# Modulation sums: 32x32 turns on VectorE and stacked identities in place of TensorE transposes, gates through DRAM, small rows on GpSimd's queue

## The chip, the cores and the metric

One core of one Trainium2 chip runs the kernel. The time is the device time of one execution in microseconds (us), median of the runs; the profile is of one further execution. Engines: PE is TensorE, PEld its weight loads, DVE is VectorE, ACT is ScalarE, POOL is GpSimd, SP is SyncE, which here only issues transfers (DMAs).

## The reference

Two blocks on a sequence of 256 rows of 1024 columns, fp32. The first is a gated mixer (a short convolution and a forgetting attention) with a feed-forward part. The second has two layers (block-wise attention, then differential attention, each with a feed-forward part), and every layer is modulated by a vector c:

```
c_act = silu(c)                                  # 1 x 1024
for i in range(2):
    mod = c_act @ ada_w[i] + ada_b[i]            # 1024 x 6144 weights
    sh_a, sc_a, g_a, sh_f, sc_f, g_f = split(mod, 6)
    h = rms_norm(x, norm_g[i, 0]) * (1 + sc_a) + sh_a
    x = x + g_a * rms_norm(attention(h), norm_g[i, 1])
    h = rms_norm(x, norm_g[i, 2]) * (1 + sc_f) + sh_f
    x = x + g_f * rms_norm(swiglu(h), norm_g[i, 3])
```

So there are 12 modulation vectors of 1024 numbers: four shifts and four scales, wanted with one channel per partition, and four gates, wanted as a row of 1024 that is the same on all 128 partitions.

## The kernel before, in words

The kernel works on two halves of 128 rows. Weights stream through three buffers (`raws`) on SP's queue; ScalarE rounds each 128x512 piece to fp32r (`hi`), VectorE subtracts it from the original (`lo`), and TensorE makes three products per piece (`triple`, or `turned_product` in the feed-forward parts, where the weights are the stationary side). Sixteen slots hold converted pieces. The order of the work is written by a planner (`Order`): it keeps a simulated time, runs tasks that yield until a due time, and pins the instructions of each engine, and of each DMA queue, in the order in which it emits them. All matmuls and transposes are emitted by `Order.mm` (L145) and `Order.tr` (L151), all other engines' work by `Lane` (L89), all DMAs by `Order.dma` (L137).

The modulation runs beside all this (`ada`, L656): its weights come through two buffers of their own (`araws`), and VectorE accumulates weight times `c_act` into a 128x512 tile `asum`, two instructions for each of 96 pieces. After eight of them a half vector (512 columns) is summed up except over the partitions, and `ada_finish` (L623) does that. For a shift or a scale, PE transposes the four 128x128 blocks, and VectorE reduces the bank along its free axis into `fm`; for a scale a second instruction adds one and multiplies the norm gain. For a gate, the tile is split into hi and lo, which takes one of the sixteen slots, two products with a matrix of ones sum it over the partitions and spread it to all of them, and VectorE multiplies it into `gated[..].tile`, into which `load_gain` (L607) has loaded the norm gain, broadcast to all partitions. That happens twice for each vector (`cc` 0 and 1). `chain` (L552) is the consumer: it waits for the marks in `ada_done`, and its first product reads the gate's tile. There are two such gain tiles.

At the start (L479 to L500) SP loads the first half of x, the first weight tile in four pieces, the second half of x, then in `later` seven small sets of rows (c, the convolution's weights, five norm gains; 4 to 6 KB each), then the next weight tiles. The first gain rows (`first_rows`) come on ScalarE's queue. PE turns the rows to columns later (`turn_rows`). A row tile of these is one of the four `ep` tiles, which the attention heads use too. An unused tile (`PAD_END`) keeps the addresses behind it where they are.

Of the kernel before, what the change touches and what calls it, by code (L numbers as in the profile page):

```python
# [12 lines left out]
F32 = mybir.dt.float32  # L13
F32R = mybir.dt.float32r
AF = mybir.ActivationFunctionType
OP = mybir.AluOpType
AX = mybir.AxisListType
# [3 lines left out]
P = 128  # L21
D = 1024
# [11 lines left out]
STOCK = 9  # L34
ADA_START, ADA_EARLY, ADA_LATE = 30.0, 5.5, 8.0
HEADS_1, HEADS_2 = 9.0, 2.0
PAD_END = 104
FIRST_DMA, SLOW_BYTES = 1.9, 2.2e6
RATE, SLOW_RATE = 360e3, 270e3
WARM = 6  # L40
# [178 lines left out]
def block_kernel(ctx: ExitStack, tc: tile.TileContext, a: dict, onehot: bass.AP, out: bass.AP):  # L219
    nc = tc.nc  # L220
    o = Order(tc)
    A, V, G = o.A, o.V, o.G
# [4 lines left out]
    dram = ctx.enter_context(tc.tile_pool(name="dram", bufs=1, space=DRAM))  # L227

    def ring(pool, name, n, shape, dtype=F32):
        return Ring([pool.tile(shape, dtype, name=f"{name}{i}") for i in range(n)])  # L230

    def small(name, shape, dtype=F32):
        return cst.tile(shape, dtype, name=name)

    banks = ring(psum, "bank", 8, [P, 512])
    raws = ring(cst, "raw", 3, [P, 2048])
    araws = ring(cst, "araw", 2, [P, 1024])
    slots = Ring([(small(f"hi{i}", [P, 512], F32R), small(f"lo{i}", [P, 512], F32R)) for i in range(16)])
    st = ring(cst, "st", 4, [P, 528])
    ch = ring(cst, "ch", 3, [P, 512])  # L240
    ep = ring(cst, "ep", 4, [P, 384])
    gains = ring(cst, "gain", 2, [P, D])
    asum = ring(cst, "asum", 2, [P, 512])
# [119 lines left out]
    def split(hi, lo, src, after=0.0):  # L363
        t = A.activation(hi, src, AF.Copy, after=after)
        return V.tensor_sub(lo, src, hi.bitcast(F32), after=t)
# [76 lines left out]
    vec = {}  # L442

    def rows(*wanted, lane=None):
        n = sum(k for _, _, k in wanted)
        got, e, r = small(f"cols{n}", [P, n]), o.hold(ep), 0
        t = e[:n, :P]
        for name, ap, k in wanted:
            arrival = o.dma(t[r:r + k, :], ap, lane)
            vec[name] = got[:, r:r + k]  # L450
            r += k
        return got, e, arrival

    def turn_rows(got, e, arrival, mark):
        yield arrival
        n = got.shape[1]
        t = e[:n, :P]
        tp = yield from o.get(banks)
        r = o.tr(tp[:, :n], t, ident[:n, :n])
        ep.give(e, r)  # L460
        yield r
        mark.t = V.tensor_copy(got, tp[:, :n])
        banks.give(tp, mark.t)

    def load_x(h):
        for n in range(2):
            c = slice(n * 512, (n + 1) * 512)
            x_in[h][n].t = o.dma(x[h][:, c], xin[h][:, c])
# [3 lines left out]
    def stay_warm():  # L472

        b = banks.take()
        for _ in range(WARM):
# [5 lines left out]
    first_rows = rows(("mix_pre", a["norm_mix_pre"].rearrange("l (k p) -> (l k) p", p=P), 8), lane=A)  # L481
    issue_raw()
    load_x(1)
    later = rows(("c", a["c_2"].rearrange("l (k p) -> (l k) p", p=P), 8),
                 ("conv", a["conv_w"].rearrange("l t (k p) -> (l t k) p", p=P), 12),
                 ("ffn_pre", a["norm_ffn_pre"].rearrange("l (k p) -> (l k) p", p=P), 8),
                 *((("g", l, i), a["norm_g_2"][l, i].rearrange("(k p) -> k p", p=P), 8) for l in range(2) for i in (0, 2)))
    ident = small("ident", [P, P])
    make_identity(nc, ident)
    tri = small("tri", [P, P])  # L490
    nc.vector.memset(tri, 1.0)
    ones_r = small("ones_r", [P, P], F32R)
# [2 lines left out]
    nc.gpsimd.affine_select(tri, tri, pattern=[[1, P]], compare_op=OP.is_ge, fill=0.0, base=0, channel_multiplier=-1)  # L495
    mhalf = small("mhalf", [P, 1])
    nc.vector.memset(mhalf, -0.5)
    pre_mark = Mark()
    o.fill = fill
    o.now = START  # L500
# [106 lines left out]
    def load_gain(src, gain):  # L607
        gain.tile = yield from o.get(gains)
        gain.load.t = o.dma(gain.tile, src.to_broadcast([P, D]))


    fm = [small(f"fm{l}", [P, 4, 8]) for l in range(2)]
# [3 lines left out]
    ada_done = {one: [Mark(), Mark()] for one in ada_order}  # L616
    gated = {one: Gain() for one in ada_order if one[1][0] == "g"}
# [2 lines left out]
    c_mark = Mark()  # L620
    c_act = small("c_act", [P, 8])

    def ada_finish(l, what, cc, sums, r):  # L623
        yield r
        c = slice(cc * 512, (cc + 1) * 512)
        if what[0] == "g":
            yield from o.until(gated[l, what].load)
            pair = yield from o.get(slots)
            hv, lv = pair
            r = split(hv, lv, sums)  # L630
            asum.give(sums, r)
            yield r
            tp = yield from o.get(banks)
            o.mm(tp, ones_r, hv, True, False)
            r = o.mm(tp, ones_r, lv, False, True)
            slots.give(pair, r)
            yield r
            dst = gated[l, what].tile[:, c]
            r = V.tensor_mul(dst, dst, tp)
        else:  # L640
            tp = yield from o.get(banks)
            for j in range(4):
                r = o.tr(tp[:, j * P:(j + 1) * P], sums[:, j * P:(j + 1) * P], ident)
            asum.give(sums, r)
            yield r
            i = {"sh_a": 0, "sc_a": 1, "sh_f": 2, "sc_f": 3}[what]
            dst = fm[l][:, i, cc * 4:cc * 4 + 4]
            r = V.reduce_sum(dst, tp.rearrange("p (k c) -> p k c", c=P), axis=AX.X)
            if what[1] == "c":
                yield r  # L650
                g = vec["g", l, 0 if what == "sc_a" else 2][:, cc * 4:cc * 4 + 4]
                r = V.scalar_tensor_tensor(dst, dst, 1.0, g, op0=OP.add, op1=OP.mult)
        banks.give(tp, r)
        ada_done[l, what][cc].t = r

    def ada():  # L656
        yield from o.until(c_mark)
        pieces = [(l, what, cc, k0) for l, what in ada_order for cc in range(2) for k0 in range(0, 8, 2)]
        loaded, t0 = [], o.now
        for i in range(len(pieces) + 1):  # L660
            if i < len(pieces):
                l, what, cc, k0 = pieces[i]
                c0 = parts_of.index(what) * D + cc * 512
                if k0 == 0:
                    if what[0] == "g" and cc == 0:
                        o.spawn(load_gain(a["norm_g_2"][l, 1 if what == "g_a" else 3].unsqueeze(0), gated[l, what]))
                    sums = yield from o.get(asum)
                    r = G.memset(sums, 0.0)
                    yield r
                    ba = o.dma(sums[0:1, :], a["ada_b_2"][l:l + 1, c0:c0 + 512])  # L670
                t = yield from o.get(araws)
                arrival = o.dma(t.rearrange("p (k c) -> p k c", c=512),
                                a["ada_w_2"][l].rearrange("(k p) c -> p k c", p=P)[:, k0:k0 + 2, c0:c0 + 512])
                loaded.append((l, what, cc, k0, t, max(arrival, ba), sums))
            if i:
                l, what, cc, k0, t, arrival, s = loaded.pop(0)
                yield max(arrival, t0 + i * ADA_EARLY)
                while (o.urgent or V.free > o.now + SLACK or
                       pos["lo"] - pos["first"] < STOCK and o.now < t0 + i * ADA_LATE):
                    yield o.now + 0.2  # L680
                for k in range(2):
                    r = V.scalar_tensor_tensor(s, t[:, k * 512:(k + 1) * 512], c_act[:, k0 + k:k0 + k + 1], s,
                                               op0=OP.mult, op1=OP.add)
                    yield r - 0.3
                araws.give(t, r)
                if k0 == 6:
                    o.spawn(ada_finish(l, what, cc, s, r), r)


    def scope(**kinds):  # L690

        stack, got = ExitStack(), {}
        for name, (n, shape, dtype) in kinds.items():
            got[name] = ring(stack.enter_context(tc.tile_pool(name=name, bufs=1, reuse_waits="tile")), name, n, shape, dtype)
        return stack, got
# [77 lines left out]
        yield from rstd(rs0[h], parts)  # L773
        rs_mark[h].t = V.tensor_scalar(rsq[h], rs0[h], 0.125, None, op0=OP.mult)

    o.spawn(turn_rows(*first_rows, pre_mark))
    for h in range(2):
        o.spawn(turn_x(h))

# [5 lines left out]

    small("pad_end", [P, PAD_END])
    phase, sc = scope(qp=(4, [P, 4, 256], F32), gp=(8, [P, 512], F32),
# [203 lines left out]
    for k0 in (0, 4):  # L991
        for h in range(2):
            t = product(b0[h], hT, h, range(k0, k0 + 4), us_0[k0:k0 + 4], hm, k0 == 0, k0 == 4)
# [5 lines left out]
    group(take(2), 260, keep_gb, None)  # L999
    o.spawn(gates_of_c())  # L1000
    o.spawn(ada(), ADA_START)
    group(take(2), 512, keep_gc, None)
    group(take(2), 512, make_z, None)
# [30 lines left out]
    for n in range(2):  # L1034
        us = take(1)
        o.wait(ya_mark)
        for h in range(2):
            ps = o.hold(banks)
            t = product(ps, yaT, h, range(4), us)
# [22 lines left out]
    for h in range(2):  # L1062
        for n in range(2):
            ps = o.hold(banks)
            t = product(ps, ybT, h, range(4), ub[n])
# [366 lines left out]
```

## Time and profile before

| what | value |
|---|---|
| median of 3 runs (lowest to highest) | 979.92 us (978.97 to 983.75) |
| the profiled execution's own time, its span | 979.98 us, 978.3 us |
| PE, PEld, DVE, ACT, POOL busy | 968.3, 808.5, 771.0, 619.5, 34.8 us |
| mean granted TensorE clock | 0.999 |
| bytes moved by DMA | 227.23 MB, 232 GB/s |

A busy share is an average over stages. Matmuls are pipelined, so the durations of neighbours overlap; what one costs is seen in the distance between starts. An x2 behind a row says that two equal instructions were merged into it. A name such as `bank<-hTb,hi` is the tile written and the tiles read.

### The profile page before, as it was taken

The numbers are of one execution on the slowest core, as the hardware profiler recorded it, in microseconds if no ns is written. First come the engines' busy times: TensorE is split into PE (matmuls) and PEld (weight loads), VectorE is DVE, ScalarE is ACT, GpSimd is POOL, SyncE is SP. The second block draws the span as 40 slices with busy tenths as digits, with TensorE's granted clock in tenths as the row PEclk, the third lists the DMA queues.
The fourth block names the chain that finished last, engine by engine and source line by source line (L and its number), as shares of the span: only waits on it lengthen the run. The fifth ranks groups of instructions, "written<-read, shape, count | busy, mean of one in ns | idle before, by whom it ended". The sixth has DMA issues, their size and how long they took to land.

```text
span 978.3 us, 14495 instructions
## 1 busy us (share of the span) xinstructions
PE 968.3 (99%) x4986; PEld 808.5 (83%) x4986; DVE 771.0 (79%) x1582; ACT 619.5 (63%) x1390; POOL 34.8 (4%) x65
## 2 busy tenths in 40 slices
PE   9999999999999999999999999999999999999997
PEld 6888778888888888888878888888887888888886
DVE  6789789889999977886899989957686787565642
ACT  6756676775555647776775555547788796564631
POOL 1000000000000001000000000001000100000000
PEclk9999999999999999999999999999999999999999
DMA  7977787679988985866769998954442567646501
GB/s 248 343 240 262 260 280 249 217 232 321 350 289 283 300 269 198 278 214 185 246 217 331 307 327 280 315 202 165 171 161 86 185 203 256 217 158 214 166 23 44
DMA packets 143637, 227.23 MB, mean 232 GB/s; under 512 B 6087, under 2 KB 79028, under 8 KB 143564
## 3 DMA queue, kind: packets, MB, share of 16 engines
q1 hardware_dynamic: 143548, 226.30, 69.3%
q8 instruction: 39, 0.64, 0.3%
q14 instruction: 34, 0.28, 0.1%
q10 hardware_dynamic: 16, 0.00, 0.0%
HBM read 225.22 MB, written 2.63 MB: 233 GB/s over the span
## 4 chain that ended last, share of the span: by engine, by line
PE 89%; DMA 4%; DVE 2%; issue 2%; ACT 1%; SPq 0%; POOL 0%; DVEq 0%; POOLq 0%; ACTq 0%
PE bank L145 85%; PE bank L151 4%; DMA raw<-in_w_gate_up_dram 1%; DMA araw<-in_ada_w_dram 1%; DMA raw<-in_w_down_dram 1%; DVE asum L89 1%; ACT hi L89 1%; DMA x<-in_x_dram 1%; DVE lo L89 1%; SPq L137 0%; DVE st L89 0%; DMA raw<-in_w_in_dram 0%; DVE wp L89 0%; DVE x L89 0%; ACT junk L89 0%
## 5 line engine op out<-in xcount | busy, mean ns | idle before, releaser
L89 DVE TENSOR_TENSOR lo<-raw,hi 128x512 fp32r<-128x512 f32 (+1 forms) x494 | 320.8, 677 | 28.6 <-ACT hi L89 24.5
L89 ACT ACTIVATE hi<-raw 128x512 fp32r<-128x512 f32 (+1 forms) x494 | 289.6, 619 | 49.1 <-PE bank L145 20.5
L145 PE MATMUL bank<-hi,hTb 128*128 128x512 f32 (+1 forms) x840 | 265.6, 389 | 0.5 <-ACT hTb L89 0.5
L145 PE MATMUL bank<-hTb,hi 128*128 128x512 f32 x640 | 203.8, 397 | 0.1
L145 PEld LDWEIGHTS bank<-hi,hTb 128*128 128x128 f32 x840 | 153.9, 188 | 30.7 <-issue 1.5
L145 PE MATMUL bank<-lo,hTb 128*128 128x512 f32 (+1 forms) x420 | 163.2, 389 | 0.0
L145 PE MATMUL bank<-hi,pair 128*128 128x512 f32 x496 | 162.5, 392 | 0.0
L89 DVE SCALAR_TENSOR_TENSOR asum<-araw,c_act,asum 128x512 f32<-128x512 f32 x192 | 143.1, 746 | 2.3 <-DMA araw<-in_ada_w_dram 2.1
L145 PEld LDWEIGHTS bank<-hTb,lo 128*128 128x128 f32 x640 | 119.9, 188 | 27.8 <-issue 0.3
L145 PE MATMUL bank<-hTb,lo 128*128 128x256 f32 x640 | 127.2, 280 | 0.0
L145 PEld LDWEIGHTS bank<-hi,pair 128*128 128x128 f32 x496 | 92.7, 188 | 18.6 <-issue 0.2
L89 ACT ACTIVATE wp<-raw 128x512 fp32r<-128x512 f32 x150 | 90.0, 626 | 24.8 <-PE bank L145 16.6
L89 ACT ACTIVATE st<-bank 128x256 f32<-128x256 f32 (+1 forms) x104 | 36.3, 397 | 106.1 <-PE bank L145 105.6
L145 PEld LDWEIGHTS bank<-hTb,hi 128*128 128x128 f32 x640 | 99.8, 189 | 3.2 <-issue 1.0
L89 DVE TENSOR_TENSOR wp<-raw,wp 128x512 fp32r<-128x512 f32 x150 | 98.8, 685 | 3.8 <-ACT wp L89 3.8
L145 PE MATMUL bank<-hTb,wp 128*128 128x512 f32 (+1 forms) x512 | 97.8, 337 | 0.0
L145 PE MATMUL bank<-lo,pair 128*128 128x512 f32 x248 | 97.3, 392 | 0.0
L145 PEld LDWEIGHTS bank<-hTb,wp 128*128 128x128 f32 x512 | 81.5, 188 | 11.5
L145 PEld LDWEIGHTS bank<-lo,hTb 128*128 128x128 f32 x420 | 79.0, 188 | 14.3 <-issue 0.5
L145 PE MATMUL bank<-wp,pair 128*128 128x512 f32 x336 | 84.5, 391 | 0.0
L89 DVE TENSOR_TENSOR st<-st,bank 128x256 f32<-128x256 f32 x96 | 39.8, 416 | 42.5 <-ACT st L89 42.4
L145 PEld LDWEIGHTS bank<-wp,pair 128*128 128x128 f32 x336 | 61.9, 188 | 12.1
(133 smaller groups left out, 868.9 us busy)
## 6 DMA issues: line engine op xcount, KB each, us to landing
araw<-in_ada_w_dram SPq DMA_DIRECT2D x96, 512.0 KB
raw<-in_ffn_w_in_dram SPq DMA_DIRECT2D x88, 512.0 KB
raw<-in_w_gate_up_dram SPq DMA_DIRECT2D x44, 512.0 KB
raw<-in_ffn_w_out_dram SPq DMA_DIRECT2D x22, 1024.0 KB
raw<-in_w_in_dram SPq DMA_DIRECT2D x16, 1024.0 KB
raw<-in_moba_w_qkv_dram SPq DMA_DIRECT2D x12, 1024.0 KB
raw<-in_diff_w_qkv_dram SPq DMA_DIRECT2D x12, 1024.0 KB
raw<-in_w_down_dram SPq DMA_DIRECT2D x11, 1024.0 KB
```

The source lines that it names most:

```text
L89: self.order.pin(self, fn(out, *args, **kw))
L145: self.pin(self.pe, self.nc.tensor.matmul(out, lhsT, rhs, start=start, stop=stop, skip_group_check=shared))
L151: self.pin(self.pe, self.nc.tensor.transpose(out, src, ident))
```

## The change

`ada_finish` now collects both halves of a vector. VectorE turns every 32x32 block of the 128x512 sum in place of its block (`transpose` into a tile of the ring `st`) and reduces the 32 columns of every block: that leaves 16 columns per half, and in a tile `fold` of 32 columns the sums over each quarter of 32 partitions. When both halves are there, four small products sum the quarters. For a shift or a scale the stationary side is `stacked` (four identities of 32x32 above one another, built at the start by four copies) and the moving side eight columns of `fold`; the result has the channels on the partitions. For a gate, the sides are exchanged, the result is eight rows of 128. These are multiplied by the norm gain's eight rows (loaded into an `ep` tile), written to a DRAM tile `gate_d`, and read back, broadcast to all partitions, into the gain tile. `load_gain` is not called for gates any more, and for the gates no slot and no ones are used. There is one `fold` tile, so one vector is in it at a time.

The seven small loads of `later` go to GpSimd's queue and stand behind the making of the identity and the masks; `turn_rows` of the first gain rows is due at once and no longer at the planner's arrival of the load. `PAD_END` goes from 104 to 40 for the 64 columns of `stacked` and `fold`.

```diff
-PAD_END = 104
+PAD_END = 40
...
-    later = rows(("c", a["c_2"].rearrange("l (k p) -> (l k) p", p=P), 8),
...
     ident = small("ident", [P, P])
     make_identity(nc, ident)
+    stacked = small("stacked", [P, 32])
+    for q in range(4):
+        nc.vector.tensor_copy(stacked[q * 32:(q + 1) * 32], ident[q * 32:(q + 1) * 32, q * 32:(q + 1) * 32])
...
     nc.vector.memset(mhalf, -0.5)
+    later = rows(("c", a["c_2"].rearrange("l (k p) -> (l k) p", p=P), 8),
+                 ("conv", a["conv_w"].rearrange("l t (k p) -> (l t k) p", p=P), 12),
+                 ("ffn_pre", a["norm_ffn_pre"].rearrange("l (k p) -> (l k) p", p=P), 8),
+                 *((("g", l, i), a["norm_g_2"][l, i].rearrange("(k p) -> k p", p=P), 8) for l in range(2) for i in (0, 2)),
+                 lane=G)
...
+    folded = Ring([(small(f"fold{i}", [P, 32]), Mark(), Mark()) for i in range(1)])
+    fold_of = {}
+    gate_d = dram.tile([4, D], F32, name="gate_d")
+
     def ada_finish(l, what, cc, sums, r):
         yield r
-        c = slice(cc * 512, (cc + 1) * 512)
+        if not cc:
+            fold_of[l, what] = yield from o.get(folded)
+            for m in fold_of[l, what][1:]:
+                m.t = None
+        while (l, what) not in fold_of:
+            yield o.now + 0.1
+        one = fold_of[l, what]
+        z = yield from o.get(st)
+        r = V.transpose(z[:, :512], sums)
+        asum.give(sums, r)
+        yield r
+        r = V.reduce_sum(one[0][:, cc * 16:(cc + 1) * 16], z[:, :512].rearrange("p (b j) -> p b j", j=32), axis=AX.X)
+        st.give(z, r)
+        one[1 + cc].t = r
+        if not cc:
+            return
+        yield from o.until(*one[1:])
+        by_q = one[0].rearrange("p (k q) -> p q k", q=4)
         if what[0] == "g":
-            yield from o.until(gated[l, what].load)
-            pair = yield from o.get(slots)
-            hv, lv = pair
-            r = split(hv, lv, sums)
...
-            o.mm(tp, ones_r, hv, True, False)
-            r = o.mm(tp, ones_r, lv, False, True)
...
-            r = V.tensor_mul(dst, dst, tp)
+            e = yield from o.get(ep)
+            row = e[:8, :P]
+            yield o.dma(row, a["norm_g_2"][l, 1 if what == "g_a" else 3].rearrange("(k p) -> k p", p=P)) + 1.0
+        tp = yield from o.get(banks)
+        for q in range(4):
+            c = slice(q * 32, (q + 1) * 32)
+            if what[0] == "g":
+                r = o.mm(tp[:8, c], by_q[:, q], stacked, True, True)
+            else:
+                r = o.mm(tp[c, :8], stacked, by_q[:, q], True, True)
+        folded.give(one, r)
+        yield r
+        if what[0] == "g":
+            i = (0 if what == "g_a" else 1) + 2 * l
+            r = V.tensor_mul(row, tp[:8, :P], row)
+            banks.give(tp, r)
+            yield r + 3.0
+            r = o.dma(gate_d[i:i + 1].rearrange("o (k p) -> (o k) p", p=P), row)
+            ep.give(e, r)
+            yield r + 6.0
+            gain = gated[l, what]
+            gain.tile = yield from o.get(gains)
+            r = o.dma(gain.tile, gate_d[i:i + 1].to_broadcast([P, D]))
         else:
-            tp = yield from o.get(banks)
-            for j in range(4):
-                r = o.tr(tp[:, j * P:(j + 1) * P], sums[:, j * P:(j + 1) * P], ident)
...
             if what[1] == "c":
+                r = V.scalar_tensor_tensor(fm[l][:, i], tp[:, :8], 1.0, vec["g", l, 0 if what == "sc_a" else 2],
+                                           op0=OP.add, op1=OP.mult)
+            else:
+                r = V.tensor_copy(fm[l][:, i], tp[:, :8])
+            banks.give(tp, r)
+        for m in ada_done[l, what]:
+            m.t = r
...
-                    if what[0] == "g" and cc == 0:
-                        o.spawn(load_gain(a["norm_g_2"][l, 1 if what == "g_a" else 3].unsqueeze(0), gated[l, what]))
...
-    o.spawn(turn_rows(*first_rows, pre_mark))
+    o.spawn(turn_rows(*first_rows[:2], o.now, pre_mark))
```

## Rows read from the trace of the kernel before

**Rows 1.** Page, part 1: busy us (share of the span) xinstructions.
```profile
PE 968.3 (99%) x4986; PEld 808.5 (83%) x4986; DVE 771.0 (79%) x1582; ACT 619.5 (63%) x1390; POOL 34.8 (4%) x65
```

**Rows 2.** Page, part 4: the chain that ended last, by engine.
```profile
PE 89%; DMA 4%; DVE 2%; issue 2%; ACT 1%; SPq 0%; POOL 0%; DVEq 0%; POOLq 0%; ACTq 0%
```

**Rows 3.** Waits of PE: waited for, us in total, times, longest.
```profile
PE bank L476 <- DVE junk L470: 1.3, 1, 1.3
PE bank L151 <- DVE st L89: 0.6, 1, 0.6
```

**Rows 4.** Timeline of PE: start, us, engine line op out<-in shapes.
```profile
325.97 0.60 PE L151 MATMUL bank<-ident,asum 128*128 128x128 f32 x4
...
327.11 0.63 PE L145 MATMUL bank<-hTb,hi 128*128 128x512 f32 x2
...
327.80 0.63 PE L145 MATMUL bank<-hTb,hi 128*128 128x512 f32 x2
```

**Rows 5.** Timeline of PE around a gate's products with ones.
```profile
593.43 0.62 PE L145 MATMUL bank<-hTb,hi 128*128 128x512 f32 x2
...
594.60 0.63 PE L145 MATMUL bank<-hTb,wp 128*128 128x512 f32 x2
```

**Rows 6.** Groups by line and form: busy us, mean ns, idle before.
```profile
L151 PE MATMUL bank<-ident,asum 128*128 128x128 f32 x64 | 9.6, 273 | 0.6 <-DVE st L89 0.6
L145 PE MATMUL bank<-hi,ones_r 128*128 128x512 f32 x8 | 3.2, 395 | 0.0
L89 DVE TENSOR_REDUCE fm<-bank 128x4 f32<-128x512 f32 x16 | 11.0, 688 | 3.1 <-PE bank L151 2.9
L89 DVE TENSOR_TENSOR lo<-asum,hi 128x512 fp32r<-128x512 f32 x8 | 5.5, 691 | 5.1 <-ACT hi L89 4.8 <-PE bank L145 0.4
L89 DVE TENSOR_TENSOR gain<-gain,bank 128x512 f32<-128x512 f32 x8 | 5.5, 682 | 1.2 <-PE bank L145 1.2
```

**Rows 7.** Timeline of PE, fp32 products with 8 moving columns.
```profile
38.88 0.28 PE L145 MATMUL bank<-logf,ones_r 128*128 128x8 f32 x2
39.02 0.37 PE L145 MATMUL bank<-logf,tri 128*128 128x8 f32 x2
39.25 0.48 PE L145 MATMUL bank<-hi,hTb 128*128 128x512 f32 x1
```

**Rows 8.** Timeline of PE, fp32 products with 128 moving columns.
```profile
760.60 1.05 PE L145 MATMUL bank<-gp,ptp 128*128 128x128 f32 x8
761.41 0.48 PE L145 MATMUL bank<-hi,hTb 128*128 128x512 f32 x1
```

**Rows 9.** Windows: stretch, us, busy us of PE, PEld, DVE, ACT, POOL; clock, DMA.
```profile
200.00:350.00 150.00, 149.66 (x791) 127.62 (x789) 138.21 (x254) 86.24 (x184) 3.69 (x7) 1.00 0.89 300
500.00:650.00 150.00, 149.91 (x790) 127.81 (x789) 139.14 (x253) 87.12 (x184) 3.16 (x6) 1.00 0.88 298
```

**Rows 10.** Timeline of DVE: a gate's last product, its first reader.
```profile
608.64 0.68 DVE L89 TENSOR_TENSOR gain<-gain,bank 128x512 f32<-128x512 f32 x1
...
774.43 0.68 DVE L89 TENSOR_TENSOR ch<-bank,gain 128x512 f32<-128x512 f32 x1
```

**Rows 11.** Timeline of SP's queue at the start.
```profile
5.48 0.27 SPq L137 DMA_DIRECT2D ep<-in_norm_ffn_pre_dram  x1
6.84 2.26 SPq L137 DMA_DIRECT2D ep<-in_norm_g_dram  x4
9.46 2.81 SPq L137 DMA_DIRECT2D raw<-in_w_in_dram  x6
```

**Rows 12.** Timeline of the start; in brackets idle before, and what ended it.
```profile
5.22 0.17 DVE L89 COPY cols<-bank 128x8 f32<-128x8 f32 x1 [3.76 <-PE bank L151]
...
12.26 0.63 ACT L89 ACTIVATE hi<-raw 128x512 fp32r<-128x512 f32 x1 [0.73 <-DMA raw<-in_w_in_dram]
...
13.86 0.50 PE L145 MATMUL bank<-hi,hTb 128*128 128x512 f32 x1 [0.54 <-ACT hTb L89]
```

**Rows 13.** Timeline of POOL at the start.
```profile
14.10 0.66 POOL L89 TENSOR_TENSOR rs<-tiny,mhalf 128x1 f32<-128x1 f32 x1 [10.47 <-DVE tiny L89]
```

More of the change, by code (lines that the diff above doesn't have):

```diff
@@ L483, in block_kernel @@
     load_x(1)
-    later = rows(("c", a["c_2"].rearrange("l (k p) -> (l k) p", p=P), 8),
-                 ("conv", a["conv_w"].rearrange("l t (k p) -> (l t k) p", p=P), 12),
-                 ("ffn_pre", a["norm_ffn_pre"].rearrange("l (k p) -> (l k) p", p=P), 8),
-                 *((("g", l, i), a["norm_g_2"][l, i].rearrange("(k p) -> k p", p=P), 8) for l in range(2) for i in (0, 2)))
     ident = small("ident", [P, P])
     make_identity(nc, ident)
+    stacked = small("stacked", [P, 32])
+    for q in range(4):
+        nc.vector.tensor_copy(stacked[q * 32:(q + 1) * 32], ident[q * 32:(q + 1) * 32, q * 32:(q + 1) * 32])
     tri = small("tri", [P, P])
@@ L621, in block_kernel @@
     c_act = small("c_act", [P, 8])
+    folded = Ring([(small(f"fold{i}", [P, 32]), Mark(), Mark()) for i in range(1)])
+    fold_of = {}
+    gate_d = dram.tile([4, D], F32, name="gate_d")
     def ada_finish(l, what, cc, sums, r):
         yield r
-        c = slice(cc * 512, (cc + 1) * 512)
-        if what[0] == "g":
-            yield from o.until(gated[l, what].load)
-            pair = yield from o.get(slots)
-            hv, lv = pair
-            r = split(hv, lv, sums)
-            asum.give(sums, r)
-            yield r
-            tp = yield from o.get(banks)
-            o.mm(tp, ones_r, hv, True, False)
-            r = o.mm(tp, ones_r, lv, False, True)
-            slots.give(pair, r)
-            yield r
-            dst = gated[l, what].tile[:, c]
-            r = V.tensor_mul(dst, dst, tp)
-        else:
-            tp = yield from o.get(banks)
-            for j in range(4):
-                r = o.tr(tp[:, j * P:(j + 1) * P], sums[:, j * P:(j + 1) * P], ident)
-            asum.give(sums, r)
-            yield r
+        if not cc:
[16 more added lines that the diff above has]
+        by_q = one[0].rearrange("p (k q) -> p q k", q=4)
+        if what[0] == "g":
+            e = yield from o.get(ep)
[21 more added lines that the diff above has]
+            r = o.dma(gain.tile, gate_d[i:i + 1].to_broadcast([P, D]))
+        else:
@@ L646, in ada_finish @@
             i = {"sh_a": 0, "sc_a": 1, "sh_f": 2, "sc_f": 3}[what]
-            dst = fm[l][:, i, cc * 4:cc * 4 + 4]
-            r = V.reduce_sum(dst, tp.rearrange("p (k c) -> p k c", c=P), axis=AX.X)
             if what[1] == "c":
[L650 to L654, printed above, removed]
+                r = V.scalar_tensor_tensor(fm[l][:, i], tp[:, :8], 1.0, vec["g", l, 0 if what == "sc_a" else 2],
+                                           op0=OP.add, op1=OP.mult)
+            else:
+                r = V.tensor_copy(fm[l][:, i], tp[:, :8])
```

## The prediction

> **What bounds the kernel now.** I read four views in this order. The page's first part: TensorE (PE) is busy in 968.3 of 978.3 us, VectorE (DVE) in 771.0 [rows 1]. A busy PE can hide gaps, since its matmuls are pipelined and their ends modelled, so I looked at its waits: the largest one after the start is 0.6 us, on a vector result [rows 3]. Then the chain that ended last: 89% of it is PE [rows 2]. Then PE's timeline, where I look at distances between starts: in the feed-forward part one step of two 512-column and two 256-column products takes 327.80 - 327.11 = 0.69 us, and the next step starts at once [rows 4]. So the time is the sum of what PE issues, and an instruction taken off PE is worth its issue time unless another engine becomes late. The profiled execution took 979.98 us (span 978.3, 1.7 around it), 0.06 over the median of 979.92; the sum below starts from it.
>
> **Taken off PE.** The 24 half sums (512 columns each) of the modulation end in two ways today.
> - Sixteen shift and scale halves are turned by four full transposes, 64 in all [rows 6]. One group starts at 325.97, and the second step behind it starts at 327.11; the one step between them takes 0.69, so the group costs 327.11 - 325.97 - 0.69 = 0.45 us [rows 4]. 16 x 0.45 = 7.2 us.
> - Eight gate halves are summed and spread by two 512-column products with ones, eight pairs [rows 6]. The step that holds such a pair lasts 594.60 - 593.43 = 1.17 us, 0.69 without it [rows 4, 5]: 0.48 each, 8 x 0.48 = 3.8 us.
> Together 11.0 us off PE. The waits of PE for these sums (0.6 us, [rows 3]) go too, but the new ones below replace them.
>
> **Put on PE.** Each of the 12 vectors gets four small fp32 products. An fp32 product is two passes: the two-product sum over the gates of the forget heads shows as x2 and x2 [rows 7]. So 12 x 4 x 2 = 96 passes. No row has these shapes (32 stationary columns with 8 moving, or 8 with 32). Bounds: four passes with 128 stationary and 8 moving columns take 39.25 - 38.88 = 0.37 us, 0.093 each [rows 7]; eight with 128 and 128 take 761.41 - 760.60 = 0.81, 0.10 each [rows 8]. That 8 moving columns cost almost as much as 128 says that the stationary side sets it. If it goes down with its columns, 32 of 128 give 0.025. Ends: 96 x 0.025 = 2.4 us and 96 x 0.10 = 9.7 us. I take 0.05 a pass, 4.8 us, because both sides shrink at least fourfold against [rows 8], and leave half of the saving to a floor per instruction.
> The Trainium skill, "TensorE: Matmul & The Clock Gate", section "LDWEIGHTS (loading the stationary operand)", says that a weight load lasts its columns over 1.2 GHz, whatever the rows; that fits the nearness of [rows 7] to [rows 8]. By it a 32-column load is an estimated 27 ns and the sum would end 2.2 us lower, at 971.3.
> Net for PE: -11.0 + 4.8 = -6.2 us.
>
> **VectorE.** It loses 16 reductions from PSUM (0.688), 8 subtractions (0.691) and 8 gain products (0.682), 22.0 us [rows 6]. It gets 24 transposes and 24 reductions of 512 columns; the nearest row is the reduction, 0.69 [rows 6], so 33.1 us, and 12 last steps of 8 or 128 columns at about 0.2 (a copy of 8 columns is 0.17, [rows 12]), 2.4. Net +13.5 us, 0.56 per half. Cover: in 200-350 us it idles 150 - 138.2 = 11.8 us, in 500-650 us 10.9 [rows 9]; with 24 halves over some 590 us about six fall in such a stretch, +3.4 us. That fits, so I cost it at nothing on the path; uncovered it would be the 13.5. The transposes have no row: at one column per cycle as the reduction 0.69, and only at (11.8 - 3.4)/6 = 1.4 us more each is the idle time gone. ScalarE loses eight conversions; it isn't late here.
> The new chain has one VectorE step more between the sum and PE (turn, reduce, then the product), and PE is in program order: whatever stands behind the small product waits too. Before there were 24 such meetings and about 0.6 us of wait [rows 3]; now 12 behind a busier engine. +0.5 us, between 0 and 3.
>
> **The gate's way through DRAM.** One small load, one 4 KB store and the broadcast load per gate, on SP's queue. The store waits there for VectorE and the broadcast for the store's landing; behind them stand the weight loads. The broadcast is the same 512 KB as the one it replaces. Slack: the tightest gate, layer 1's first, is multiplied last at 608.64 and first read at 774.43 [rows 10], 166 us for a trip that is a handful of load times. What might cost is a stalled SP: four gates; the three weight buffers and sixteen converted slots hide a few us each. Zero, up to 2 us for all four. The row's tile is one of four that the attention heads use too, and is held for the trip; a head that finds none starts later, at worst by the trip, and is counted in those 2 us.
>
> **The start.** Seven small loads leave SP. Today SP issues the third of them at 5.48 and the last four at 6.84 and after, spread over 2.26 us, and the second weight tile only at 9.46 [rows 11]. ScalarE then waits 0.73 us for that tile at 12.26, the activation's conversion is queued behind it, and PE idles 0.54 us at 13.86 [rows 12]. From there PE runs without gaps, so the start is worth what PE idles. Freed of the seven, SP can issue the tile at about 5 us, so the 0.54 goes. The 8 gain rows are also turned ahead of x instead of behind; VectorE copies them at 5.22 today [rows 12] and x's first eviction follows: some 0.3 us. -0.8 us; ends 0 and -1.5. GpSimd must issue seven loads before its next work, due at 14.10 after 10.47 us of idleness [rows 13]; at up to 1.5 us each they fit, no row shows its price. Behind that instruction stands the scale of the first half's evictions. c and the other rows are read after 30 us.
> The Trainium skill, "DMA: Bandwidth & Descriptors", section "Issuing engines are not separate DMA queues", speaks against this part: other issuing engines save only the sequencer's issue time. By it the tile would land little earlier and the sum would be 0.5 us higher, 974.0; [rows 11] show more than issue time, gaps between SP's issues.
>
> **Sum.** 979.98 - 11.0 + 4.8 + 0.5 - 0.8 = 973.5 us.
>
> **The rivals.**
> 1. The small passes cost like wide ones. For it: 0.093 with only 8 moving columns [rows 7]. Against: their stationary side is 128. 9.7 instead of 4.8: 978.4, no change.
> 2. VectorE becomes the bound (the other side). From a turn of 2.1 us on, 1.4 over the reduction's 0.69, the idle time of 200-350 and 500-650 us [rows 9] is gone and converted weights come late. At 3.1 us a turn each stretch lacks 6 x 1.0 = 6 us, both 12: 985.5, slower. For it: VectorE is 92% busy there, and turning fp32 has no row. Against: each operation of 512 columns in [rows 6] takes 0.68 to 0.69, whatever it does.
> 3. The change moves waits: SP blocked by the stores, GpSimd's seven loads late, 4 us together: 977.5, no change.
> 4. Passes at the low end, 2.4, and the start at -1.5: 970.4.
>
> **How the numbers follow.** A measurement of this kernel tells 0.5% (4.9 us) from no change: below 975.0 is faster, above 984.8 slower. The forecast (971.5 to 975.5) has 0.60, of it 0.05 above 975.0. Rival 1 has 0.17, rival 3 0.06, both no change; rival 2 0.08, of it 0.07 slower and 0.01 no change; rival 4 0.09, faster. Faster 0.55 + 0.09 = 0.64, same 0.05 + 0.17 + 0.06 + 0.01 = 0.29, slower 0.07. For 8 in 10 the range holds the forecast, rival 4's 970.4 and rivals 1 and 3 up to 978.4 with a wait or two: 969.5 to 979.5.
>
> **What would show it.** Right: no transposes of the sums and no products with ones on PE; 96 passes at distances near 0.05 us; 24 turns near 0.7 us; PE's list of waits still under about 4 us; the second weight tile issued near 5 us. Wrong: passes near 0.1 us; turns over 1.5 us with PE waiting for converted weights in 200-350 us; SP waiting for a gate's store while weights are due; GpSimd busy past 14 us.

## The result and the profile after

The changed kernel takes 972.63 us (971.90 to 973.88), the kernel before in the same session 980.38 (978.97 to 983.75). The ratio is 0.9918, 95% interval 0.9904 to 0.9931: 6.8 to 9.4 us less. (A sixth run, at 1194 us under a granted clock of 0.752, counts in the median but is in neither the span given nor the ratio.) The forecast was 973.5. The profiled execution took 972.75 us, 7.2 less than the one before. The page, part 1:

```profile
PE 961.5 (99%) x5002; PEld 800.6 (82%) x5002; DVE 781.2 (80%) x1606; ACT 612.1 (63%) x1382; POOL 39.4 (4%) x72
```

Against [rows 1], PE is busy 6.8 us less, with 16 instructions more, and VectorE 10.2 us more. PE's waits stay few; the new set of products waits once, 0.5 us, in the place of the 0.6 in [rows 3]:

```profile
PE bank L476 <- DVE junk L470: 1.3, 1, 1.3
PE bank L145 <- DVE logf L89: 0.6, 1, 0.6
PE bank L145 <- DVE fold L89: 0.5, 1, 0.5
PE bank L145 <- DVE lo L89: 0.5, 2, 0.2
```

The groups that stand where those of [rows 6] stood (line engine op, out<-in, xcount | busy us, mean ns | idle before):

```profile
L145 PE MATMUL bank<-fold,stacked 128*32 128x8 f32 x64 | 2.0, 186 | 0.5 <-DVE fold L89 0.5
L145 PE MATMUL bank<-stacked,fold 128*8 128x32 f32 x32 | 1.6, 194 | 0.0
...
L89 DVE STREAM_TRANSPOSE st<-asum 128x512 f32<-128x512 f32 x24 | 16.9, 703 | 0.0
L89 DVE TENSOR_REDUCE fold<-st 128x16 f32<-128x512 f32 x24 | 16.3, 677 | 0.0
```

The 96 passes are there (64 and 32), and the turn takes 0.703 us where 0.69 was assumed. What a set of passes costs PE is read from distances again. Around a shift's set, and around a gate's:

```profile
230.72 0.39 PE L145 MATMUL bank<-lo,pair 128*128 128x512 f32 x1
231.04 0.25 PE L145 MATMUL bank<-fold,stacked 128*32 128x8 f32 x8
231.22 0.73 PE L145 MATMUL bank<-hi,pair 128*128 128x512 f32 x2
231.79 0.40 PE L145 MATMUL bank<-lo,pair 128*128 128x512 f32 x1
...
232.49 0.39 PE L145 MATMUL bank<-lo,pair 128*128 128x512 f32 x1
```

```profile
313.79 0.39 PE L145 MATMUL bank<-lo,pair 128*128 128x512 f32 x1
314.01 0.61 PE L145 MATMUL bank<-hi,pair 128*128 128x512 f32 x2
314.56 0.41 PE L145 MATMUL bank<-stacked,fold 128*8 128x32 f32 x8
314.90 0.50 PE L145 MATMUL bank<-lo,pair 128*128 128x512 f32 x1
315.24 0.40 PE L145 MATMUL bank<-hi,pair 128*128 128x512 f32 x1
```

One lo and two hi products take 232.49 - 231.79 = 0.70 us; with the shift's set between them 231.79 - 230.72 = 1.07, so the set costs 0.37. With the gate's set it is 314.90 - 313.79 = 1.11, and the lo behind it takes 0.34 where 0.23 is usual: 0.41 + 0.11 = 0.52. Worked out in this way over every set that stands among plain products, the medians are 0.40 and 0.55: 8 x 0.40 + 4 x 0.55 = 5.4 us, predicted 4.8. And 5.4 is not 96 equal prices: the eight passes of a shift occupy only 231.22 - 231.04 = 0.18 us of their 0.37.

The start, SP's queue, then PE and GpSimd (POOL):

```profile
4.56 15.18 SPq L137 DMA_DIRECT2D raw<-in_w_in_dram  x9
```

```profile
13.63 0.40 PE L145 MATMUL bank<-lo,hTb 128*128 128x512 f32 x1
13.87 0.62 PE L145 MATMUL bank<-hi,hTb 128*128 128x512 f32 x2
```

```profile
4.37 2.04 POOL L137 DMA_DIRECT2D ep<-in_norm_g_dram  x4
...
11.44 0.56 POOL L89 TENSOR_TENSOR rs<-tiny,mhalf 128x1 f32<-128x1 f32 x1 [3.91 <-DVE tiny L89]
```

The second weight tile is issued at 4.56 instead of 9.46 [rows 11], PE no longer idles at 13.86 [rows 12], and GpSimd, at about 0.5 us a load, has issued its seven loads at 6.41 and still idles 3.91 us ahead of the work of [rows 13].

### The profile page after: what moved, and what is told of

The parts are those of the page before. It is cut to its first block, busy times and chain, and to the rows that moved or that the text cites. A ratio compares the mean times of both kernels' runs of the same rounds, so it can differ in the third digit from the quotient of the medians.

```text
span 971.0 us, 14500 instructions
## 1 busy us (share of the span) xinstructions
PE 961.5 (99%) x5002; PEld 800.6 (82%) x5002; DVE 781.2 (80%) x1606; ACT 612.1 (63%) x1382; POOL 39.4 (4%) x72
## 4 chain that ended last, share of the span: by engine, by line
PE 91%; DVE 2%; issue 2%; DMA 2%; ACT 2%; POOL 0%; DVEq 0%; POOLq 0%; SPq 0%; ACTq 0%
PE bank L145 87%; PE bank L151 4%; ACT hi L89 1%; DMA raw<-in_ffn_w_out_dram 1%; DMA bf<-in_b_f_dram 1%; DVE lo L89 1%; DMA raw<-in_ffn_w_in_dram 0%; DVE ch L89 0%; ACT junk L89 0%; PE bank L476 0%; POOL tiny L89 0%; DVE x L89 0%; ACT wp L89 0%; DVE asum L89 0%; DVE st L89 0%
## 5 line engine op out<-in xcount | busy, mean ns | idle before, releaser
L89 DVE TENSOR_TENSOR lo<-raw,hi 128x512 fp32r<-128x512 f32 (+1 forms) x478 | 310.5, 674 | 25.2 <-ACT hi L89 21.7
L89 ACT ACTIVATE hi<-raw 128x512 fp32r<-128x512 f32 (+1 forms) x478 | 278.0, 618 | 67.2 <-PE bank L145 20.4
L145 PE MATMUL bank<-hi,hTb 128*128 128x512 f32 (+1 forms) x812 | 253.8, 387 | 0.1
L145 PE MATMUL bank<-hTb,hi 128*128 128x512 f32 x576 | 183.1, 397 | 0.0
L145 PE MATMUL bank<-hi,pair 128*128 128x512 f32 x524 | 172.6, 392 | 0.0
L145 PEld LDWEIGHTS bank<-hTb,lo 128*128 128x128 f32 x576 | 107.8, 188 | 25.0 <-DVE asum L89 0.3
L145 PE MATMUL bank<-hTb,wp 128*128 128x256 f32 (+1 forms) x640 | 121.6, 337 | 0.0
L145 PEld LDWEIGHTS bank<-hTb,wp 128*128 128x128 f32 x640 | 102.3, 188 | 14.9
L145 PE MATMUL bank<-hTb,lo 128*128 128x256 f32 x576 | 114.5, 280 | 0.0
L145 PEld LDWEIGHTS bank<-hTb,hi 128*128 128x128 f32 x576 | 89.5, 189 | 1.9 <-issue 0.7
```

What stands on the lines that cost most here:

```text
L89: self.order.pin(self, fn(out, *args, **kw))
L145: self.pin(self.pe, self.nc.tensor.matmul(out, lhsT, rhs, start=start, stop=stop, skip_group_check=shared))
```

## Experiments

Differences are worked out from the ratio of the runs, times 980.4, with the interval in brackets.

**The sums without the start, and the start alone.** The first undoes the start in the changed kernel, the second makes it alone in the kernel before.

```diff
-    later = rows(..., lane=G)                  # behind the masks
+    later = rows(...)                          # on SP, ahead of ident
-    o.spawn(turn_rows(*first_rows[:2], o.now, pre_mark))
+    o.spawn(turn_rows(*first_rows, pre_mark))
```

> All of the change but its start: the small rows go back to SyncE's queue in their old place and the 8 gain rows are turned behind x as before. Theory of the sum (11.0 us of PE work off, the new small products on at 0.40 us a set of shift or scale and 0.55 us a set of gate, as the trace after shows, 8 x 0.40 + 4 x 0.55 = 5.4): 5.6 us less than before, some 974.5. Rival, that the small products are not what the gain is and the start carries more of it: 3 us less or under. Rival, that the start is worth nothing: as the changed kernel, 7 to 7.5 us less.

> The start alone: the kernel before with its small rows on GpSimd's queue, issued behind its masks, and the 8 gain rows turned first. Theory: PE's 0.54 us of idleness at 13.86 us goes, and a part of a microsecond ahead of the first product; 0.6 to 0.8 us less than before. The rule of the Trainium skill that issuing engines are not separate queues: 0. Rival, the start carries more than the sum gave it: 1.5 us less or more.

Measured: the sums alone 973.07 us, -7.2 [-8.4, -5.9]; the start alone 979.81, -0.6 [-1.6, +0.4]. The two add up to the whole. The 5.6 us expected of the sums is a little less than the interval allows; the next runs ask where the rest is.

**Shift and scale alone; gates alone.** Each keeps the other's old end, and the old start.

```diff
 def ada_finish(l, what, cc, sums, r):
     yield r
+    if what[0] == "g":     # first run; != "g" in the second
+        ...                # the old end of this half
+        return
```

> Shift and scale by turns and small products, gates with ones and the start as before. Theory: 16 groups of four transposes at 0.45 us go, 8 sets of four products at 0.40 us come: 7.2 - 3.2 = 4.0 us less than before. By the price of the prediction (0.05 us a pass, 64 passes) the same 4.0. Rival, a set costs as much as a group of transposes: 7.2 - 3.6 = 3.6; a set whose fixed cost is shared: up to 5.5 less. VectorE as the bound: no gain.

> Gates as eight rows by way of DRAM, shift and scale by the transposes of the whole sums and the start as before. Theory by sets: 8 pairs at 0.48 us go, 4 sets at 0.55 us come: 3.8 - 2.2 = 1.6 us less than before. By the prediction's price a pass (32 passes at 0.05): 3.8 - 1.6 = 2.2 less. Rival, the way through DRAM stalls SyncE's queue by about 0.5 us a gate: no gain, or slower by up to 0.4.

Measured: shift and scale 976.07, -3.7 [-5.0, -2.5], as worked out. Gates 976.92, -2.9 [-4.0, -2.0]: the 2.2 of the prediction is inside, the 1.6 by sets is not.

**No end of the gates at all.** In the kernel before, the gates' conversion, products and multiplication are left out.

```diff
         if what[0] == "g":
             yield from o.until(gated[l, what].load)
+            asum.give(sums, r)
+            for m in ada_done[l, what]:
+                m.t = gated[l, what].load.t
+            return
             ...                # the old end, not reached any more
```

> The kernel before without the end of the gates: no conversion, no products with ones, no multiplication; the gain tile keeps the normalisation's gain alone. What is left out is the gates of the modulation. It measures what the old end of the gates cost in full. Theory of the sum: eight pairs at 0.48 us, 3.8 us less than before, 976.7. Rival, that the converted-weight slots and ScalarE's and VectorE's steps cost as well: 5 us less or more, 975.5 or under; with the 2.9 us that the new gates alone gained, a new set with its way through DRAM would then cost 2.1 us or more in all.

Measured: 975.77, -4.8 [-6.1, -3.4]. By the best estimates the old end of the gates cost a microsecond more than its products with ones (3.8), and the new end costs 4.8 - 2.9 = 1.9 us, which the four sets (4 x 0.52) fill; nothing is left over for the way through DRAM. But the interval holds the 3.8 as well, so the microsecond is not shown by this run alone. A part of it may be seen in the traces: PE's wait of 0.6 us of [rows 3], at 350 us (2.0 and 0.9 in the two runs that change the start alone), is in neither this trace nor that of the gates alone. What else it is stays open.

**Five times the products.**

```diff
-        for q in range(4):
+        for q in list(range(4)) * 5:
```

> The changed kernel with each set's four small products emitted five times over into the same place: 16 more products a set, 32 more passes, 384 in all (256 with 8 moving columns, 128 with 32). It tells a fixed cost of a set from a price of a pass. Fixed cost: the trace after has these passes 0.01 us (8 columns) and 0.03 us (32 columns) apart, so 256 x 0.01 + 128 x 0.03 = 6.4 us more than the changed kernel's 972.6, some 979. Price of the prediction, 0.05 a pass: 19.2 more, 992. Price of a whole set, 0.40 and 0.55 us for eight passes: 12.8 + 8.8 = 21.6 more, 994.

Measured: 983.04, 10.4 more than the changed kernel. Two sets of this run on PE's timeline:

```profile
231.04 0.52 PE L145 MATMUL bank<-fold,stacked 128*32 128x8 f32 x40
231.49 0.74 PE L145 MATMUL bank<-hTb,wp 128*128 128x512 f32 x3
...
314.62 1.34 PE L145 MATMUL bank<-stacked,fold 128*8 128x32 f32 x40
315.89 0.50 PE L145 MATMUL bank<-hTb,hi 128*128 128x512 f32 x1
```

Forty passes of a shift take 0.45 us where eight took 0.18: (0.45 - 0.18) / 32 = 0.008 each. Those of a gate take 1.27 against 0.34: 0.029 each. So 256 x 0.008 + 128 x 0.029 = 5.8 us are the passes, and what is left of a set's 0.37 and 0.52, some 0.3 us, is paid once a set: for these narrow passes the fixed cost is shown, and 0.05 a pass is refuted. The other 4.6 are not passes. About half is one wait in layer 1's attention, which the next runs explain; 2 us I could not place.

**Shift and scale in one set.** The two vectors of a half-layer share a folded tile of 64 columns.

```diff
-                r = o.mm(tp[c, :8], stacked, by_q[:, q], True, True)
+                r = o.mm(tp[c, :16], stacked, by_q[:, q], True, True)   # once, at the scale
```

> A further step: shift and scale of one half-layer share a folded tile, and one set of four products with 16 moving columns does both; 4 sets of shift and scale in the place of 8. Theory: a set costs a fixed 0.40 us, so 4 x 0.40 = 1.6 us less than the changed kernel, 971.0. Rival, the set's cost goes with its moving columns (16 instead of 8): no change, 972.6. Rival, the shift that waits for its scale comes late to the feed-forward part: longer by what PE's waits then show.

Measured: 974.12, -6.4 [-7.6, -5.2], 1.5 slower than the changed kernel by the medians, though the intervals of the ratios overlap. The sets of 16 columns cost about 0.4, so the fixed price held and four were saved; something else ate it. PE at the end of layer 1's attention, here and in the changed kernel:

```profile
756.37 2.84 PE L145 MATMUL bank<-gp,ptp 128*128 128x128 f32 x24
...
760.42 0.39 PE L145 MATMUL bank<-hi,pair 128*128 128x512 f32 x1
762.77 1.25 PE L151 MATMUL bank<-ident,st 128*128 128x128 f32 x8 [1.96 <-DVE st L89]
```

```profile
754.68 2.94 PE L145 MATMUL bank<-gp,ptp 128*128 128x128 f32 x24
...
760.67 0.39 PE L145 MATMUL bank<-hi,pair 128*128 128x512 f32 x1
760.90 0.60 PE L151 MATMUL bank<-ident,st 128*128 128x128 f32 x4
761.25 0.48 PE L145 MATMUL bank<-hi,pair 128*128 128x512 f32 x1
```

The last heads' values (gp, ptp) go through eight squares on ScalarE, a power on GpSimd and a product on VectorE before PE turns them (ident, st). The changed kernel's planner put 15 large products in between, this one 7, and PE waits 1.96 us. Adding up how far PE's starts lie beyond what the same instructions take elsewhere, 750 to 775 us loses 0.3 us in the kernel before, 0.8 in the changed one, 3.3 here and 3.2 with five times the products (7 as well).

**The same pairs in two other orders.** Each run changes one number of the planner.

```diff
-ADA_START, ADA_EARLY, ADA_LATE = 30.0, 5.5, 8.0
+ADA_START, ADA_EARLY, ADA_LATE = 30.0, 5.3, 8.0   # first run
-STOCK = 9
+STOCK = 8                                         # second run
```

> The pairs of the last experiment but with the modulation's pieces due every 5.3 us in the place of 5.5, a number that moves the planner's order alone. The pairs' trace lost 3.3 us of PE in 750 to 775 us, where 7 products stand between the last head's values and the transposes of their result, and the transposes waited 2.0 us for VectorE; the changed kernel has 15 products there and lost 0.8. With 5.3 the order has 15 products again. Theory, that the pairs' saving (4 sets at 0.40) was eaten by this wait: 2 to 2.5 us less than the pairs, 971.5 to 972.0, and at or a little under the changed kernel. Rival, 16 moving columns make a set dearer: it stays at 974.

> The pairs with another number of the planner: an accumulation may start once eight converted weights are in stock, in the place of nine. Its order at the end of layer 1's attention is that of the kernel before: the first transposes of the values' result stand 4 products behind the values, the second ones 23 products further on. Theory, that PE's loss in 750 to 775 us is set by the products that stand between the values and the transposes (23: 0.3 us; 15: 0.8 to 1.4; 7: 3.3; 3: 5.4): 0.3 us there, 3 us less than the pairs, 971 us, 1.5 less than the changed kernel. Rival, the loss belongs to VectorE's load (the accumulations moved earlier here, into the feed-forward part of layer 0): no better than the pairs, 974, with waits for converted weights in 500 to 650 us.

Measured: 971.84, -9.7 [-11.2, -8.1], and 971.58, -8.8 [-11.0, -6.7]. The medians are 2.3 and 2.5 us under the pairs, where the losses differ by 1.9 and 3.1; the first interval is clear of the pairs', the second overlaps it, and there the trace has to show it. The second run's order at that place:

```profile
755.95 1.95 PE L145 MATMUL bank<-gp,ptp 128*128 128x128 f32 x16
...
758.66 0.60 PE L151 MATMUL bank<-ident,st 128*128 128x128 f32 x4
...
764.35 0.60 PE L151 MATMUL bank<-ident,st 128*128 128x128 f32 x4
```

Four products stand ahead of the first transposes and 23 between the two groups, neither waits, and the stretch loses 0.2 us. The first run (15 products) loses 1.4. These two are the lowest medians of the study. That they beat the changed kernel, by about 1 us, is not shown: the intervals of the ratios overlap.

**More turns on VectorE.** The cover that the prediction counted on is taken away in two doses.

```diff
-        r = V.transpose(z[:, :512], sums)
+        for _ in range(4):                 # 2 in the second run
+            r = V.transpose(z[:, :512], sums)
```

> The changed kernel with each half's turn on VectorE issued four times: 72 more of 0.70 us, 50.6 us more VectorE work, 2.1 us more a half. It takes away the cover that the prediction gave VectorE. By rival 2 of the prediction the cover ends at 1.4 us more a half, then 12 halves in the two dense stretches cost (2.1 - 1.4) each: 8.4 us more, 981. Theory of the traces: the accumulations wait for a free VectorE and slide into emptier stretches (the last one from 638 us before to 738 after), VectorE is idle for some 190 us of the span and the tightest gate has 100 us of slack: 0 to 1.5 us more, 972.6 to 974.1. If nothing can slide, all 50.6 us show: 1023.

> The changed kernel with each half's turn issued twice: 24 more turns, 16.9 us more VectorE work. With four turns (50.6 us more) layer 1's attention gate came 143 us later (its broadcast was issued at 807 us instead of 664) and PE waited 29.4 us for what hangs on it. Theory: the slide is about three times the work added, 48 us here, and the gate's slack is 102 us; so nothing of the 16.9 shows, 0 to 1 us more, and 2 to 3 more from the order at the end of layer 1's attention (3 products between the values and the transposes of their result): 973 to 976. Rival, VectorE's work shows as it is added (45.7 of 50.6 us did): 15 us more, 988.

Measured: 1018.34 and 979.17 us, 45.7 and 6.5 more than the changed kernel. My theory failed in both. With four turns (PE's waits; SP's queue; VectorE):

```profile
PE bank L151 <- DVE ch L89: 30.2, 3, 29.4
PE bank L145 <- DVE fold L89: 7.1, 1, 7.1
```

```profile
807.06 0.34 SPq L137 DMA_DIRECT2D gain<-gate_d  x1
```

```profile
812.12 0.69 DVE L89 TENSOR_TENSOR ch<-bank,gain 128x512 f32<-128x512 f32 x1 [0.46 <-DMA gain<-gate_d]
```

The dense stretches are not where it shows. The planner holds the accumulations back while VectorE is busy, and up to a latest time while fewer than nine converted weights are in stock, so the work slid, as I had said; but it slid past a due date. Layer 1's attention gate was issued at 807.06, in the changed kernel at 664.51 with its first reader at 767.07 (SP's queue and VectorE there are shown below), and everything behind that residual step waited.

```profile
664.51 0.46 SPq L137 DMA_DIRECT2D gain<-gate_d  x1
```

```profile
767.07 0.68 DVE L89 TENSOR_TENSOR ch<-bank,gain 128x512 f32<-128x512 f32 x1
```

Two waits of 36.5 us are most of the 45.7; behind this idleness PE's granted clock is 0.71 in 800 to 850 us, a mix of its two levels (1.2 and 2.4 GHz), and more is lost there.

With two turns the gate's broadcast is issued at 722.52, still in time for its reader at 771.89, and 4.6 of the 6.5 us (5.4 against 0.8) are lost in 750 to 775 us, where 3 products were left:

```profile
763.39 0.66 PE L151 MATMUL bank<-ident,st 128*128 128x128 f32 x4 [1.20 <-DVE st L89]
765.88 0.55 PE L145 MATMUL bank<-hi,pair 128*128 128x512 f32 x1 [1.83 <-ACT pair L89]
```

The expectation named that order and its place, but priced it at 2 to 3 us.

**The start's order without another queue.**

```diff
+    issue_raw()
     later = rows(...)                          # on SP, behind the masks
```

> The start's order without another queue: the kernel before, its seven small loads still issued by SyncE but behind the second weight tile, and the 8 gain rows turned first. It tells whether the early weight tile is a matter of order or of GpSimd's queue. Order: the tile is issued at about 5 us, PE's 0.54 us of idleness at 13.9 is gone, 0.6 us less than before as with GpSimd's queue. Queue: the tile still waits, no change. The time alone can hardly tell; the issue times and PE's idleness in the first 25 us can.

Measured: 979.61, -1.9 [-2.8, -0.9]. SP's queue:

```profile
4.70 2.81 SPq L137 DMA_DIRECT2D raw<-in_w_in_dram  x4
7.82 0.35 SPq L137 DMA_DIRECT2D ep<-in_c_dram  x1
```

The tile leaves at 4.70 and the 0.54 us are gone: it is order, not a second queue. That agrees with the rule of the Trainium skill, "DMA: Bandwidth & Descriptors", section "Issuing engines are not separate DMA queues", which the prediction had weighed against this part: what moving the loads saves is SP's time ahead of the tile, and SP can save it itself. Whether -1.9 here and -0.6 for the start alone differ is not shown: the intervals overlap. The traced execution of the start alone took 982.72 us, the longest of its twelve, and PE waits in it at two places:

```profile
38.74 0.36 PE L145 MATMUL bank<-logf,tri 128*128 128x8 f32 x2 [1.17 <-DVE logf L89]
352.01 1.11 PE L151 MATMUL bank<-ident,asum 128*128 128x128 f32 x4 [2.00 <-DVE st L89]
```

The kernel before waits 0.52 and 0.62 at these places. Over all traces the wait for logf lies between nothing and 1.4 us with the small loads on SP's queue and between nothing and 1.2 with them on GpSimd's, so it is no price of GpSimd's queue that these runs can show.

## Why the prediction came out, step by step

- **Off PE, 11.0.** For shift and scale it holds: 7.2 less 8 sets at 0.40 is 4.0, measured 3.7. For the gates it was probably low: 3.8 against 4.8 [3.4, 6.1] for the whole old end, and the gates alone gained 2.9 [2.0, 4.0] where 3.8 less four sets at 0.55 leaves 1.6.
- **On PE, 4.8.** The sum was nearly right (5.4), its split wrong. The step that failed is the floor "per instruction": the floor is one price per set, 0.3 us, and the passes themselves cost 0.008 and 0.029, not 0.05; the distances near 0.05 that were to show the forecast right did not come. My 0.05 split the fixed price over eight passes, by luck. The reading of [rows 7] behind it, "the stationary side sets it", is not what failed. Of those four passes the first two take 39.02 - 38.88 = 0.14 us and the second two 39.25 - 39.02 = 0.23, 0.11 a pass, near the 0.10 of [rows 8]: with 128 stationary columns each pass has its price, whether 8 or 128 columns move. What failed with it is that the price "goes down with its columns": passes with 32 cost 0.008 and passes with 8 cost 0.029. Rival 1 fell by its own "against": these passes have fewer stationary columns than 128, and none costs 0.1. By the Trainium skill's page "TensorE: Matmul & The Clock Gate", section "LDWEIGHTS (loading the stationary operand)", a 32-column load is an estimated 27 ns and an 8-column one 7; the prediction took the 27 for all 96 passes. The trace disagrees with both, with 8 ns a pass at 32 stationary columns and 29 at 8.
- **VectorE costs nothing.** Right for the change: the turn is 0.703, and VectorE's 10.2 us more (13.5 were reckoned) show in few waits (the next point). But the cover was misread. I measured it as idle time of two stretches and put its end at 1.4 us more a half; with 0.7 more a half 6.5 us were already lost, 4.6 of them at one place outside both stretches. The cover is the slack to the next due date and the order of the work around it: the change alone moved the last accumulation from 637.9 to 737.8 us, into layer 1's attention. How far it moves is the planner's rule as much as VectorE's load: with the pairs the last accumulation starts at 719.9 us when nine converted weights must be in stock and at 631.4 when eight must, with the same work on VectorE. Rival 2 has the right sign of more VectorE work, at the wrong place.
- **Waits, +0.5.** One wait of 0.5 for a folded sum, two of 0.2 for `lo`, and the 0.6 of [rows 3] gone. Unforeseen: 0.5 at the end of layer 1's attention, where the planner's new order stands; other orders of nearly the same work lose from 0.2 to 5.4 there.
- **The gate's trip, 0.** Right: layer 1's first gate is issued at 664.51 and read at 767.07, 103 us later, where [rows 10] had 166.
- **The start, -0.8.** Measured -0.6 [-1.6, +0.4], an interval that holds 0 as well as -0.8; the tile's issue near 5 us and PE's 0.54 came as named.

The forecast was 0.9 us too high; as a saving, 6.5 us, it lies just under the measured 6.8 to 9.4. The sum of the measured pieces, 3.7 + 2.9 + 0.6 = 7.2 us less, lies inside. By the best estimates the gates' old end is the term furthest off (3.8 for 4.8), but its interval does not exclude the 3.8.

## What to carry over

Price small narrow products by the set, not by the pass: a set of eight passes with 32 or 8 stationary columns cost some 0.3 us before its passes, and the passes little, so put more into a set before you make its passes smaller. With 128 stationary columns it was the other way round, 0.11 us for each pass. One price per pass, taken as the mean of a short group, hides which of the two you have; read the distances inside the group. When a planner holds work back until an engine is free, the cover of that engine ends at the first due date that the work slides past, not where its idle time is used up; look up the due dates. And a plan that is remade by any edit carries its own few microseconds, so look first at the places where a long chain must be covered before a run is taken as the price of the edit.

## Not expected of the hardware

- Small fp32 passes followed one another at 0.008 us (32 stationary, 8 moving columns) and at 0.029 us (8 and 32). Moving columns would explain it; so would the place of the results, since a shift's four products write four different groups of 32 partitions and a gate's the same eight. Sixteen moving columns (the pairs) did not raise a set's 0.40 visibly, which speaks for the second; it was not tried by itself.
- What the 0.3 us of a set are, whether the change of type or the next weights that no long product hides, stays open. The rows of the changed kernel show where they fall, in three parts of about 0.1 each: the long product ahead of a set takes 0.32 to the set's first pass instead of 0.23 (231.04 - 230.72), of the 0.18 of a shift's eight passes 8 x 0.008 leaves 0.11, and the first long product behind a set takes 0.34 instead of 0.23 (315.24 - 314.90).
- A small load costs GpSimd about 0.5 us of its own time to issue (four in 2.04), about as much as SP's four in 2.26 [rows 11].
